# Seven-product weight sums formed by adding transfers in device memory instead of on VectorE, in all four feed-forward layers of a diffusion backbone step

## The chip, the cores and the metric

One core of one Trainium2 chip runs the whole step as one program. The metric is the device time of one execution in microseconds (us); lower is better. Engines are named as in the profile: PE (TensorE matmul), PEld (its weight loads), DVE (VectorE), ACT (ScalarE), POOL (GpSimd) and SP (SyncE, which issues nearly all transfers). Each engine works through its own queue in order and waits at the head of the queue for semaphores of the others.

## The reference

Two layers, 640 tokens (128 context, 512 latent) of width 1024, all in fp32. Each layer is a half-step SwiGLU feed-forward, a mixer (layer 0: a two-dimensional DFT, "Fourier"; layer 1: neighbourhood attention), and a second half-step feed-forward; every part has a norm and a modulation before and after.

```python
def _swiglu(h, w1, w2):
    gate, up = jnp.split(h @ w1, 2, axis=-1)
    return (jax.nn.silu(gate) * up) @ w2

def _half_ffn(x, m, k, g_pre, g_post, w1, w2):
    h = _modulated_prenorm(x, g_pre, m, k)
    return x + 0.5 * m[:, 3 * k + 2, None] * _rmsnorm(_swiglu(h, w1, w2), g_post)

def _fourier_mix(h, w_in, w_out):
    b, s, _ = h.shape
    u = (h @ w_in).reshape(b, s, N_FOURIER_GROUPS, FOURIER_GROUP_DIM)
    f = jnp.fft.fft2(u.astype(jnp.float32), axes=(1, 3), norm="ortho").real
    return f.astype(h.dtype).reshape(b, s, D_MODEL) @ w_out
```

The modulation is `silu(cond) @ w_mod[i] + b_mod[i]`, 2 x 9216 columns over a depth of 1024. D_FF is 2816, 22 "f tiles" of 128.

## The kernel before

**Order of the work.** The program is straight-line: six sub-layers n = 0 to 5, of which n = 0, 2, 3 and 5 are the feed-forward layers (`ffn`), n = 1 is the Fourier mixer (`fourier`) and n = 4 the attention. A list `units` holds all weight tiles (128 x 1024 fp32, 512 KB) in the order of use. `unit(i)` sends up to unit i+3: `send` issues a load on SP into one of four `raw` buffers and splits it into a `hi` part (ACT, line 260) and a `lo` part (DVE, line 261), in six pairs of `hi`/`lo` buffers. Every product is three matmul passes (`mm3`, lines 274 to 276).

**Seven products.** For most f tiles (`w1_fast`) the product of the hidden states with the gate and up columns is formed in Winograd's manner: the weights are four 512-column blocks (two of the gate, two of the up, called `one` and `two` in the code), the tokens two halves, and seven block products take the place of eight. `combine` forms the sums on the token side once per layer. The weight sums are formed for each f tile on DVE inside `send`: kinds `"sums"` and `"again"` by three additions of 512 columns (lines 228 to 230), kind `"all"` by one more (line 243). The gate and the up tile stay in `raw` buffers from their load to their last sum. After every four fast tiles a slice of the second matrix follows (`w2`, five token tiles).

**Background jobs.** The modulation columns are 128 jobs (`gemv`, line 478): one load of 512 KB and two DVE instructions each. `BEHIND` says how many run after `w2` passes of a layer (36, 0, 36, 36, 0, 8); 4 more run in the last slice of n = 0 and 8 inside `fourier` (three in `pair_in(1)`, five between `channels`).

**Fourier.** Its input and output weights are folded on DVE as they are loaded (lines 237 and 238, 16 units). Position sums and channel sums alternate on PE (`positions`, `channels`), each with its split on ACT and DVE between them.

Of the kernel before, what the change touches and what calls it, by code (L numbers as in the profile page):

```python
# [18 lines left out]
P = 128  # L19
# [24 lines left out]
BEHIND = (36, 0, 36, 36, 0, 8)  # L44
TURNS = (
# [107 lines left out]
class Kernel:  # L153
# [59 lines left out]
    def send(self, kind, src):  # L213
# [18 lines left out]
        elif kind.startswith("fold"):  # L232
            raw = self.raw_tile(src)
            a, b = raw[:, one], raw[:, two]
            if "rows" not in kind:
                a, b = a.rearrange("p (m c) -> p m c", m=4)[:, :, 2:], raw[:, 520:].rearrange("p (m c) -> p m c", m=4)
            nc.vector.tensor_tensor(b, a, b, op=ALU.subtract)
            nc.vector.scalar_tensor_tensor(out=a, in0=a, scalar=2.0, in1=b, op0=ALU.mult, op1=ALU.subtract)
        elif kind == "up":
            raw = self.fast["up"]  # L240
        else:
            raw, at = self.fast["gate"], two
            nc.vector.scalar_tensor_tensor(out=raw[:, two], in0=self.fast["sums"][:, two], scalar=-1.0,
                                           in1=raw[:, two], op0=ALU.mult, op1=ALU.subtract)
        n = at.stop - at.start
        if kind in ("block", "foldblock", "foldrowsblock"):
# [4 lines left out]
        return hi, lo  # L251

# [360 lines left out]
    def chain(self, n, i, pss, acc=()):  # L613
# [66 lines left out]
        with high():  # L680
# [33 lines left out]
            if n == 0:  # L714
                j, n_pieces = tiles[0], 2 * len(tiles)
                y = self.staged[:, 2 * j : 2 * j + n_pieces][:, :: -1 if j == CTX_TILE else 1]
# [4 lines left out]
                if i in (1, 2):  # L721
                    v, t, col = (2, SPECIAL, TOK + 1) if i == 1 else (5, 0, TOK)
                    for c in range(0, NCH, 2):
                        hi, lo = (h.block(part, c, 0)[:, :, col] for part in range(2))
                        self.split(hi, lo, self.staged[:, v, c : c + 2, t])
# [13 lines left out]
    def ffn(self, layer, which, base, boundary):  # L739
# [45 lines left out]
        def combine(step):  # L785
# [16 lines left out]
            if step < 2:  # L802
                t = combine.now[k] = [self.temp(("square", "total")[step]).rearrange(shape, **sizes) for _ in range(2)]
                steps = ((1, t[0], b12, b11), (2, t[1], b22, t[0]))
            else:
                t = combine.now[k]
                steps = ((3, t[0], b22, b12), (4, t[1], t[1], b21))
            for i, to, a, b in steps:
                if k == 0:
                    sums[i] = [quad(self.ring(F32R)) for _ in range(2)]  # L810
                nc.vector.tensor_tensor(to, a, b, op=ALU.subtract)
# [37 lines left out]
        def w1_fast(f, ahead):  # L849
# [28 lines left out]
            with high():  # L878
                tt(a, a, w, op=ALU.add)
# [10 lines left out]
            with high():  # L890
                nc.vector.scalar_tensor_tensor(out=q, in0=w, scalar=-1.0, in1=q, op0=ALU.mult, op1=ALU.subtract)
# [24 lines left out]
        def w2(s, tiles):  # L916
# [7 lines left out]
            for a0, f in [(a, f) for a in range(2) for f in range(f0, f1)] if ends else [(None, f) for f in range(f0, f1)]:  # L924
                w = self.unit(base + w2_at[s] + f - f0)
                if n == 0 and s == len(SLICES) - 1 and tiles[0] == 0 and f < f0 + 4:
# [23 lines left out]
        for op, a, half in plan:  # L950
# [7 lines left out]
            elif op == "combine":  # L958
                combine(a)
            elif op == "first":  # L960
# [809 lines left out]
```

## Time and profile before

| | before |
|---|---|
| median of 3 runs (lowest to highest) | 2219.53 us (2216.15 to 2219.59) |
| the profiled execution's own time | 2218.44 us |
| its span, first to last instruction | 2216.7 us |
| mean granted TensorE clock | 0.988 |
| moved by transfers | 293.25 MB, mean 132 GB/s |

The profiled execution lies 1.1 us under the median. Its time is 1.7 us more than its span. A busy PE is not a PE at its peak: matmuls are pipelined, and at half clock a busy PE does half the work, so the granted clock has to be read beside the busy share.

### The profile page before, as it was taken

The numbers are of one execution on the slowest core, as the hardware profiler recorded it, in microseconds if no ns is written. First come the engines' busy times: TensorE is split into PE (matmuls) and PEld (weight loads), VectorE is DVE, ScalarE is ACT, GpSimd is POOL, SyncE is SP. The second block draws the span as 40 slices with busy tenths as digits, with TensorE's granted clock in tenths as the row PEclk, the third lists the DMA queues.
The fourth block names the chain that finished last, engine by engine and source line by source line (L and its number), as shares of the span: only waits on it lengthen the run. The fifth ranks groups of instructions, "written<-read, shape, count | busy, mean of one in ns | idle before, by whom it ended". The sixth has DMA issues, their size and how long they took to land.

```text
span 2216.7 us, 34573 instructions
## 1 busy us (share of the span) xinstructions
PE 2173.2 (98%) x13299; PEld 1997.3 (90%) x13299; DVE 1743.1 (79%) x3218; ACT 1179.2 (53%) x2221; POOL 45.3 (2%) x95
## 2 busy tenths in 40 slices
PE   7999999999899999999999999999999999999998
PEld 5999999977699999898998999989998899999997
DVE  5988898889798889878998898686556686766684
ACT  4544545464654545446544454466778654455452
POOL 0000000010100000001000000010000000000000
PEclk9999999998999999999999999999999999999999
DMA  8244344625324434452344444533333323322242
GB/s 315 86 143 162 134 152 139 216 86 178 116 96 138 159 132 147 148 196 99 109 147 146 141 143 146 179 99 101 111 101 110 119 81 105 115 95 77 95 129 100
DMA packets 85861, 293.25 MB, mean 132 GB/s; under 512 B 9696, under 2 KB 14656, under 8 KB 85568
## 3 DMA queue, kind: packets, MB, share of 16 engines
q1 hardware_dynamic: 85152, 290.39, 39.1%
q8 instruction: 104, 1.70, 0.3%
q10 hardware_dynamic: 544, 0.66, 0.1%
q14 instruction: 61, 0.50, 0.1%
HBM read 275.49 MB, written 11.58 MB: 130 GB/s over the span
## 4 chain that ended last, share of the span: by engine, by line
PE 89%; DVE 5%; ACT 3%; DMA 2%; issue 1%; POOL 0%; SPq 0%; DVEq 0%; POOLq 0%; ACTq 0%
PE main L275 12%; PE main L276 12%; PE main L274 12%; PE score L275 7%; PE score L276 7%; PE score L274 7%; PE turn L275 4%; PE turn L274 4%; PE sum L274 4%; PE sum L275 4%; PE turn L276 4%; PE sum L276 4%; DVE junk L478 1%; DMA raw<-in_w_mod_t 1%; PE sum L1569 1%
## 5 line engine op out<-in xcount | busy, mean ns | idle before, releaser
L260 ACT ACTIVATE hi<-raw 128x1024 fp32r<-128x1024 f32 (+1 forms) x388 | 371.1, 969 | 287.3 <-PE score L275 93.1
L261 DVE TENSOR_TENSOR lo<-raw,hi 128x1024 fp32r<-128x1024 f32 (+1 forms) x388 | 429.7, 1112 | 99.1 <-ACT hi L260 97.7
L274 PE MATMUL main<-hi,ring 128*128 128x512 f32 (+4 forms) x1089 | 412.3, 380 | 5.9 <-ACT hi L260 2.3
L275 PE MATMUL main<-lo,ring 128*128 128x512 f32 (+4 forms) x1089 | 410.8, 378 | 4.8 <-DVE lo L261 4.8
L276 PE MATMUL main<-hi,ring 128*128 128x512 f32 (+5 forms) x1089 | 410.3, 377 | 0.0
L478 DVE SCALAR_TENSOR_TENSOR junk<-raw,wide 128x1024 bf16<-128x1024 f32 x256 | 313.1, 1223 | 79.6 <-DMA raw<-in_w_mod_t 75.5
L276 PE MATMUL score<-ring,lo 128*128 128x320 f32 x916 | 283.4, 309 | 0.6 <-DVE lo L261 0.6
L275 PE MATMUL score<-ring,hi 128*128 128x320 f32 x916 | 283.7, 310 | 0.0
L274 PE MATMUL score<-ring,hi 128*128 128x320 f32 x916 | 283.3, 309 | 0.0
L274 PEld LDWEIGHTS main<-hi,ring 128*128 128x128 f32 (+2 forms) x1089 | 204.9, 189 | 47.9 <-ACT hi L260 3.6
L275 PEld LDWEIGHTS main<-lo,ring 128*128 128x128 f32 (+2 forms) x1089 | 205.9, 189 | 43.9 <-DVE lo L261 6.3
L276 PEld LDWEIGHTS main<-hi,ring 128*128 128x128 f32 (+2 forms) x1089 | 206.0, 189 | 40.5 <-issue 1.2
L274 PE MATMUL turn<-ring,hi 128*128 128x320 f32 x672 | 207.6, 309 | 3.0 <-ACT ring L260 2.9
L275 PE MATMUL turn<-ring,hi 128*128 128x320 f32 x672 | 208.3, 310 | 0.0
L274 PE MATMUL sum<-ring,hi 128*128 128x320 f32 x672 | 208.0, 310 | 0.1
L275 PE MATMUL sum<-ring,hi 128*128 128x320 f32 x672 | 207.8, 309 | 0.0
L276 PE MATMUL sum<-ring,lo 128*128 128x320 f32 x672 | 207.5, 309 | 0.0
L276 PE MATMUL turn<-ring,lo 128*128 128x320 f32 x672 | 207.0, 308 | 0.0
L942 ACT ACTIVATE y<-main 128x512 f32<-128x512 f32 x160 | 94.2, 591 | 208.2 <-PE main L276 207.0
L274 PEld LDWEIGHTS score<-ring,hi 128*128 128x128 f32 x916 | 172.4, 188 | 1.1
L276 PEld LDWEIGHTS score<-ring,lo 128*128 128x128 f32 x916 | 172.2, 188 | 1.0 <-DVE lo L261 1.0
L275 PEld LDWEIGHTS score<-ring,hi 128*128 128x128 f32 x916 | 172.3, 188 | 0.7
(318 smaller groups left out, 4138.8 us busy)
## 6 DMA issues: line engine op xcount, KB each, us to landing
raw<-in_w SPq DMA_DIRECT2D x272, 512.0 KB, 3.7
raw<-in_w_mod_t SPq DMA_DIRECT2D x128, 512.0 KB, 3.5
raw<-in_qkv SPq DMA_DIRECT2D x26, 512.0 KB, 3.5
spill<-ring SPq DMA_DIRECT2D x12, 640.0 KB, 3.3
ring<-spill SPq DMA_DIRECT2D x12, 640.0 KB, 7.4
raw<-in_bias SPq DMA_DIRECT2D x16, 448.0 KB, 3.7
first<-in_w_mod_k SPq DMA_DIRECT2D x8, 512.0 KB, 8.2
ring<-in_w_mod_k SPq DMA_DIRECT2D x8, 512.0 KB, 10.2
```

The costliest lines, as they stand in the source:

```text
L260: a = self.nc.scalar.activation(hi, src, AF.Copy)
L261: self.last_split = a, self.nc.vector.tensor_tensor(lo, src, hi.bitcast(F32), op=ALU.subtract)
L274: mm(out, whi, xhi, start=start, stop=False)
L275: mm(out, whi, xlo, start=False, stop=False)
L276: self.latest = mm(out, wlo, xhi, start=False, stop=stop)
L478: last = self.nc.vector.scalar_tensor_tensor(out=self.junk, in0=raw, scalar=1.0, in1=self.wide[:, cond, :], op0=ALU.mult, op1=ALU.mult, ac ...
L942: nc.scalar.activation(place(i, a), ps[a], AF.Copy)
L1569: mm = nc.tensor.matmul(out, cache_v[:, ds] if k is None else v[c // 2][c % 2][:, slot, ds], probs, start=n == 0, stop=n == len(tiles) - 1)
```

## The change

For every fast tile that is not of kind `"again"` (17 in n = 0, 18 in each of n = 2, 3 and 5: 71 of 79) the four DVE additions go away. In their place POOL issues transfers within device memory: four plain copies of 512 columns (256 KB) into a scratch tensor `far`, then four transfers that add (gate + up block, up + up block, then the sum of three, then the sum of all four). A 16-byte transfer ahead of them, which reads a tile that ACT has just written, holds the group back to its place, five f tiles ahead. The loads of the sums then come from `far`: per f tile SP issues the gate tile, two sums (512 KB), two pieces of 256 KB for the up unit, and a half tile for `"all"`.

The Fourier input fold moves: eight background jobs in n = 0 load the tile, fold it on DVE and write it back through POOL, and `fourier` loads folded tiles. The eight jobs inside `fourier` go; in n = 0 one job runs after each fast tile from f = 5 on. Signs of the token sums change, a column of the context order moves so that eight small splits go away, splits inside `fourier` get high priority, one bank changes.

```diff
+FAR = (0, 2, 3, 5)
...
+        elif kind == "pieces":
+            raw = self.raw.tile([P, UNIT], F32, tag="raw", name=self.name("raw"))
+            for a, piece in zip((one, two), src):
+                nc.sync.dma_start(out=raw[:, a], in_=piece)
+        elif kind == "half":
+            raw, at = self.raw_tile(src, 512), one
...
+    def fold_in(self, k):
+
+        raw = self.raw_tile(self.io["four_in"][k])
+        a, b = (t.rearrange("p (m c) -> p m c", m=4) for t in (raw[:, :512], raw[:, 520:]))
+        self.fold(a[:, :, 2:], b)
+        self.nc.gpsimd.dma_start(out=self.folded[k], in_=raw)
+
+    def far_sums(self, n, f, stage, passed):
+
+        one, two = slice(0, 512), slice(512, UNIT)
+        w1 = self.io["w1"][n // 3, n % 3 // 2, f] if (n, f) in self.far else None
+        put, add = self.nc.gpsimd.dma_start, partial(self.nc.gpsimd.dma_start, accum_op=ALU.add)
+        while w1 is not None and self.staged_sums.get((n, f), 0) <= stage:
+            t, at = self.far[n, f].rearrange("p (a k) -> p a k", a=4), self.staged_sums.get((n, f), 0)
+            if at == 0:
+                put(out=t[:1, :, :1], in_=passed[:1, 0, :4].bitcast(F32).unsqueeze(2))
+                for a, src in enumerate((w1[0][:, one], w1[0][:, one], w1[1][:, one], w1[0][:, two])):
+                    put(out=t[:, a], in_=src)
+            elif at == 1:
+                add(out=t[:, 2], in_=w1[1][:, two])
+                add(out=t[:, 0], in_=w1[1][:, one])
+            elif at == 2:
+                add(out=t[:, 1], in_=t[:, 2])
+            else:
+                add(out=t[:, 3], in_=t[:, 1])
+            self.staged_sums[n, f] = at + 1
...
             elif op == "combine":
                 combine(a)
+                if a == 3:
+                    for stage in range(4):
+                        for f in range(7 if stage < 3 else 6):
+                            self.far_sums(n, f, stage, sums[4][0])
...
             elif op == "fast":
                 w1_fast(a, half)
+                for i in range(4):
+                    self.far_sums(n, a + 5 - i, i, g[a])
+                if n == 0 and a > 4:
+                    self.behind()
...
+                            self.units.append({"sums": ("plain", t[:, :UNIT]), "all": ("half", t[:, UNIT + 512 :]),
+                                               "up": ("pieces", (t[:, UNIT : UNIT + 512], w1[v, 1][:, 512:]))}[op])
...
-                if p and k % 3 == 1:
-                    self.behind()
...
-            self.behind((2, 2, 1, 0)[m])
...
+        for k in range(NCH):
+            self.background.insert(6 + 13 * k // 2, partial(self.fold_in, k))
```

DVE, in the middle of the last feed-forward layer (n = 5), one fast tile from its first sum with the y product to its second hidden half. Before (`sums` and `raw` are the weight tiles in fp32, `left` and `right` the results):

```order
L871 TENSOR_TENSOR left_19973<-score_18368,left_19970 128x320
L875 TENSOR_TENSOR left_20005<-left_19973,turn_19952 128x320
L261 TENSOR_TENSOR lo_20060<-raw_20057,hi_20059 128x1024
L879 TENSOR_TENSOR left_20005<-left_20005,sum_20008 128x320
L228 TENSOR_TENSOR sums_20110<-raw_20096,raw_20108 128x512
L229 TENSOR_TENSOR raw_20108<-raw_20108 128x512
L230 TENSOR_TENSOR sums_20110<-raw_20096,raw_20108 128x512
L261 TENSOR_TENSOR lo_20087<-raw_20084,hi_20086 128x1024
L886 TENSOR_TENSOR right_20006<-left_19973,turn_19952 128x320
L261 TENSOR_TENSOR lo_20099<-raw_20096,hi_20098 128x1024
```

Now:

```order
L906 TENSOR_TENSOR left_20655<-score_18966,left_20652 128x320
L910 TENSOR_TENSOR left_20687<-left_20655,turn_20633 128x320
L295 TENSOR_TENSOR lo_20742<-raw_20739,hi_20741 128x1024
L914 TENSOR_TENSOR left_20687<-left_20687,sum_20690 128x320
L295 TENSOR_TENSOR lo_20778<-raw_20775,hi_20777 128x1024
L921 TENSOR_TENSOR right_20688<-left_20655,turn_20633 128x320
L922 TENSOR_TENSOR right_20688<-right_20688,right_20653 128x320
L295 TENSOR_TENSOR lo_20790<-raw_20787,hi_20789 128x1024
```

The three additions between the splits are gone, and nothing stands in their place on DVE.

POOL, between the feed-forward layers. Before, POOL has only small powers (L610, the roots of the norms) and, in the attention, fills; this is where the attention begins:

```order
L610 TENSOR_TENSOR col_9748<-col_9748,power 128x1
L610 TENSOR_TENSOR col_9756<-col_9756,power 128x1
L1311 MEMSET rms_14462 64x128 x2
L610 TENSOR_TENSOR col_13681<-col_13681,power 128x1
L610 TENSOR_TENSOR col_13695<-col_13695,power 128x1
```

Now, in the second feed-forward layer (n = 2), the group of one f tile (`far_111`) between its neighbours, with the semaphores that each row waits for (DMASW are those of POOL's own transfers):

```order
L275 DMA far_111<-ring_7080 4x1x1 [waits Activation_49]
L284 DMA far_110<-far_110 128x512 [waits DMASW7_49,DMASW4_49]
L277 DMA far_111<-in_w 128x512 [waits DMASW0_49]
L277 DMA far_111<-in_w 128x512 x2
L277 DMA far_111<-in_w 128x512 [waits DMASW5_49]
L280 DMA far_111<-in_w 128x512 [waits DMASW2_49]
L279 DMA far_111<-in_w 128x512 [waits DMASW4_49]
L282 DMA far_111<-far_111 128x512 [waits DMASW7_49,DMASW3_49]
L284 DMA far_111<-far_111 128x512 [waits DMASW5_49,DMASW1_49,DMASW0_49]
L275 DMA far_112<-ring_7220 4x1x1 [waits Activation_49]
```

Although the code asks for one step of four different f tiles at a time, the scheduler has put the nine transfers of one f tile behind each other, each step waiting in POOL's queue for the one before it, and the next f tile's group behind them.

DVE in `fourier`, around the first position sums (`rms`, `left` and `total` are the splits that PE waits for, `lo` the splits of weights, `junk` the modulation jobs). Before:

```order
L261 TENSOR_TENSOR total_5004<-main_4995,square_5003 126x384
L478 SCALAR_TENSOR_TENSOR junk,mod<-raw_5007,wide 128x1024
L237 TENSOR_TENSOR raw_5015<-raw_5015 128x512
L478 SCALAR_TENSOR_TENSOR junk,mod<-raw_5007,wide 128x1024
L238 SCALAR_TENSOR_TENSOR raw_5015<-raw_5015 128x512
L478 SCALAR_TENSOR_TENSOR junk,mod<-raw_5011,wide 128x1024
L261 TENSOR_TENSOR left_5050<-main_5039,left_5049 128x322
L478 SCALAR_TENSOR_TENSOR junk,mod<-raw_5011,wide 128x1024
L261 TENSOR_TENSOR ring_5020<-raw_5015,ring_5019 128x1024
L261 TENSOR_TENSOR ring_4948<-score_5023,ring_4947 128x322
```

Now:

```order
L295 TENSOR_TENSOR total_5276<-main_5267,square_5275 126x384
L257 TENSOR_TENSOR raw_5279<-raw_5279 128x512
L257 TENSOR_TENSOR raw_5329<-raw_5329 128x512
L258 SCALAR_TENSOR_TENSOR raw_5279<-raw_5279 128x512
L258 SCALAR_TENSOR_TENSOR raw_5329<-raw_5329 128x512
L295 TENSOR_TENSOR left_5314<-main_5303,left_5313 128x322
L257 TENSOR_TENSOR raw_5379<-raw_5379 128x512
L295 TENSOR_TENSOR total_5326<-main_5317,square_5325 126x384
L295 TENSOR_TENSOR ring_5284<-raw_5279,ring_5283 128x1024
L295 TENSOR_TENSOR ring_5220<-score_5287,ring_5219 128x322
```

The modulation jobs are gone from between the splits; the folds of the output weights remain.

## Rows read from the trace of the kernel before

**Rows 1.** Page, part 1: busy us of each engine, share of the span.

```profile
PE 2173.2 (98%) x13299; PEld 1997.3 (90%) x13299; DVE 1743.1 (79%) x3218; ACT 1179.2 (53%) x2221; POOL 45.3 (2%) x95
```

**Rows 2.** Stretches of n = 0, 2 and 5: length, busy us, clock, DMA share, GB/s.

```profile
111.00:407.00 296.00, 296.00 (x1757) 275.70 (x1757) 262.54 (x433) 144.43 (x226) 0.00 (x0) 1.00 0.44 145
629.00:999.00 370.00, 369.94 (x2216) 345.83 (x2215) 321.89 (x526) 177.42 (x276) 0.00 (x0) 1.00 0.45 150
1855.00:2146.00 291.00, 291.00 (x1724) 270.85 (x1724) 195.16 (x304) 144.70 (x224) 0.00 (x0) 1.00 0.28 94
```

**Rows 3.** Stretches of 10 us in the Fourier mixer, same columns.

```profile
480.00:490.00 10.00, 6.95 (x25) 5.28 (x26) 9.96 (x18) 3.07 (x3) 0.00 (x0) 0.66 0.33 107
...
520.00:530.00 10.00, 8.23 (x35) 6.74 (x33) 9.97 (x18) 2.31 (x4) 0.00 (x0) 0.67 0.64 215
...
540.00:550.00 10.00, 10.00 (x27) 6.70 (x25) 9.55 (x20) 2.31 (x4) 0.00 (x0) 0.52 0.67 213
550.00:560.00 10.00, 7.65 (x26) 5.79 (x24) 7.04 (x12) 4.76 (x9) 0.00 (x0) 0.80 0.46 157
```

**Rows 4.** Timeline of PE there: start, us, instruction, [idle before, releaser].

```profile
483.05 0.58 PE L275 MATMUL main<-lo,ring 128*128 128x256 f32 x1 [3.37 <-DVE lo L261]
...
522.10 0.39 PE L274 MATMUL main<-hi,ring 128*126 128x256 f32 x1 [1.77 <-DVE rms L261]
...
539.49 0.41 PE L274 MATMUL score<-left,hi 128*128 128x322 f32 x1 [1.85 <-DVE ring L261]
```

**Rows 5.** Waits of PE, 440 to 615 us: total, times, longest.

```profile
PE main L274 <- ACT hi L260: 2.3, 1, 2.3
```

**Rows 6.** Timeline of DVE ahead of two of those stops.

```profile
510.41 1.23 DVE L478 SCALAR_TENSOR_TENSOR junk<-raw,wide 128x1024 bf16<-128x1024 f32 x1 [0.22 <-DMA raw<-in_w_mod_t]
...
537.81 1.22 DVE L478 SCALAR_TENSOR_TENSOR junk<-raw,wide 128x1024 bf16<-128x1024 f32 x1
...
538.95 0.49 DVE L261 TENSOR_TENSOR ring<-score,ring 128x322 fp32r<-128x322 f32 x1
```

**Rows 7.** Groups of DVE by line and form, whole span (count, busy, mean ns).

```profile
L228 DVE TENSOR_TENSOR sums<-raw,raw 128x512 f32<-128x512 f32 x79 | 54.4, 688 | 6.1 <-DMA raw<-in_w 5.7
...
L237 DVE TENSOR_TENSOR raw<-raw 128x504 f32<-128x504 f32 x8 | 5.3, 680 | 2.1 <-DMA raw<-in_four_in 2.1
L238 DVE SCALAR_TENSOR_TENSOR raw<-raw 128x504 f32<-128x504 f32 x8 | 5.3, 680 | 0.1
```

**Rows 8.** Timeline of ACT in n = 5: the first copy of three fast tiles.

```profile
1889.59 0.44 ACT L867 ACTIVATE left<-score 128x320 f32<-128x320 f32 x1 [0.30 <-PE score L276]
...
1901.95 0.44 ACT L867 ACTIVATE left<-score 128x320 f32<-128x320 f32 x1 [0.45 <-PE score L276]
...
1966.73 0.44 ACT L867 ACTIVATE left<-score 128x320 f32<-128x320 f32 x1 [0.22 <-PE score L276]
```

**Rows 9.** DMA issues: queue, count, KB each, median us from issue to landing.

```profile
raw<-in_w SPq DMA_DIRECT2D x272, 512.0 KB, 3.7
...
total<-gate SPq DMA_DIRECT2D x12, 256.0 KB, 3.4
...
x_out<-ring SPq DMA_DIRECT2D x8, 256.0 KB, 2.1
...
wide<-in_cond_rows SPq DMA_DIRECT2D x1, 1024.0 KB, 9.7
...
gate<-rms SPq DMA_DIRECT2D x6, 8.0 KB, 1.8
```

**Rows 10.** POOL's largest group, by line and form.

```profile
L610 POOL TENSOR_TENSOR col<-col,power 128x1 f32<-128x1 f32 x55 | 32.5, 597 | 1568.0 <-DVE col L609 1512.9 <-DVE col L607 55.0
```

**Rows 11.** The busiest 10 us of transfers in a feed-forward layer (columns of rows 2).

```profile
430.00:440.00 10.00, 10.00 (x44) 8.09 (x44) 7.04 (x13) 0.00 (x0) 0.00 (x0) 1.00 0.92 374
```

More of the change, by code (lines that the diff above doesn't have):

```diff
@@ L233, in send @@
             raw = self.raw_tile(src)
[L234 to L238, printed above, removed]
+            self.fold(raw[:, one], raw[:, two])
+        elif kind == "pieces":
[4 more added lines that the diff above has]
+            raw, at = self.raw_tile(src, 512), one
         elif kind == "up":
@@ L242, in send @@
             raw, at = self.fast["gate"], two
-            nc.vector.scalar_tensor_tensor(out=raw[:, two], in0=self.fast["sums"][:, two], scalar=-1.0,
-                                           in1=raw[:, two], op0=ALU.mult, op1=ALU.subtract)
+            nc.vector.tensor_tensor(raw[:, two], self.fast["sums"][:, two], raw[:, two], op=ALU.add)
         n = at.stop - at.start
-        if kind in ("block", "foldblock", "foldrowsblock"):
+        if kind in ("block", "foldblock"):
             hi, lo = (self.ring(F32R)[:, :n] for _ in range(2))
@@ L925, in w2 @@
                 w = self.unit(base + w2_at[s] + f - f0)
-                if n == 0 and s == len(SLICES) - 1 and tiles[0] == 0 and f < f0 + 4:
+                if n == 0 and s == len(SLICES) - 1 and tiles[0] == 0 and f < f0 + 3:
                     self.behind()
@@ L1034, in list_units @@
         self.bases = []
-        self.plans = {}
+        self.plans, self.far, self.staged_sums = {}, {}, {}
         for i in range(DEPTH):
@@ L1053, in list_units @@
                 if i == 0:
-                    self.units += [("foldblock" if k >= NWU else "fold", io["four_in"][k]) for k in range(NCH)]
+                    self.folded = [self.dram.tile([P, UNIT], F32, tag=f"fold{k}", name=self.name("fold")) for k in range(NCH)]
+                    self.units += [("block" if k >= NWU else "plain", self.folded[k]) for k in range(NCH)]
                     self.units += [("plain", io["dft"][k]) for k in range(3)]
-                    self.units += [("foldrowsblock" if u in (3, 4) else "foldrows", io["four_out"][u]) for u in range(NCH)]
+                    self.units += [("foldblock" if u in (3, 4) else "fold", io["four_out"][u]) for u in range(NCH)]
                 else:
@@ L1175, in positions @@
             p = [self.temp("left", F32R)[:, :322] for _ in range(2)]
-            self.split(*p, ps)
+            with high():
+                self.split(*p, ps)
             ps = diffs(m)
             q = [self.temp(kind, F32R)[:126, :384] for kind in ("square", "total")]
-            self.split(*q, ps)
+            with high():
+                self.split(*q, ps)
             return p, q
@@ L1251, in pair_out @@
             boundary(j, far)
+        self.unit(at + 4)
         pair_out(1)
@@ L1726, in host_inputs @@
     small = np.zeros((P, 208))
-    small[:64, :64] = -wave(np.sin, ctx, ctx, CTX) / 128
+    small[:64, :64] = -wave(np.sin, back, ctx, CTX) / 128
     small[:64, 64:128] = -small[:64, :64]
```

47 lines of the change are left out of this document (31 added, 16 removed).

## The prediction

> **What bounds the kernel now.** I read the busy shares first. PE is busy for 2173.2 of 2216.7 us, DVE for 1743.1 [rows 1]. That alone would say that taking work from DVE is worth nothing, so I went on by stretches. In the feed-forward layers PE has no gap at all: 296.00 of 296 us in n = 0, 369.94 of 370 in n = 2, 291.00 of 291 in n = 5, each at full granted clock [rows 2]. DVE is close behind in the first two (262.54 of 296, 321.89 of 370) and far behind in n = 5 (195.16 of 291), where PE is no faster for it. So there, PE is the bound, and a DVE with less to do gives nothing by itself.
>
> The Fourier mixer is the other kind of stage. Between 480 and 560 us DVE is busy for over 9.5 of 10 us in three of the four stretches shown, and PE is the one that stops [rows 3]. The timeline of PE names the stops: 3.37, 1.77 and 1.85 us, each ended by a DVE split [rows 4]. Behind each stop the granted clock falls to the lower of its two levels, 1.2 in place of 2.4 GHz, for part of the stretch: 0.66 after the first, 0.67 after the second, 0.52 and 0.80 after the third [rows 3]. A stop therefore costs twice, once idle and once in slow matmuls. Ahead of the second and third stop DVE was working through modulation jobs of 1.22 us each; the split that PE waited for from 537.6 us on began the moment such a job had ended, at 538.95 [rows 6].
>
> **What the change does to the Fourier mixer.** It takes out eight modulation jobs (16 instructions of 1.22 us, 19.5 us) and eight folds (16 of 0.68 us, 10.9 us [rows 7]): 30 us of DVE in a stage where DVE is what PE waits for. What that is worth I take from the stops, not from the 30 us:
> - Second stop: 1.77 idle, and 10 x (1 - 0.67) = 3.3 us of clock. DVE is full from 504 us on, and four job instructions of 1.22 us stand in that stretch (the row at 510.41 is one), so about 5 us ahead of the split go, more than the stop is long. I take all 5.1.
> - Third stop: 1.85 idle and 4.8 + 2.0 us of clock, a job directly ahead. I take all 8.6.
> - First stop: 3.37 idle and 3.4 us of clock. What is ahead of it on DVE is mostly work of the layer boundary, which stays; five of the folds run earlier, with a gap of DVE after them. I take 2 of 6.8.
> - One wait of 2.3 us for ACT near 560 us [rows 5]: the weight that ACT splits is folded on DVE first, and that fold stays, but DVE reaches it earlier. I take 1.3.
>
> Sum: 5.1 + 8.6 + 2 + 1.3 = 17 us. The lower bound is 0: what comes late next is the round trip PE, ACT, DVE, PE of the position sums, and if it ends where DVE's queue ended before, nothing is gained. The upper bound takes all four in full: 5.1 + 8.6 + 6.8 + 2.3 = 22.8, with some 5 us more if splits at high priority also shorten the stops too small to show here, 28.
>
> **What it does to DVE in the feed-forward layers.** 71 f tiles lose four instructions of 0.69 us [rows 7], the other three lines reading alike, 2.8 us of about 19, 196 us in all. n = 0 gains eight more modulation jobs and eight folds, 20.9 + 10.9 = 32 us, and loses 17 x 2.8 = 47. All of this lies under a full PE, so I cost it at nothing; the cover is the 33 us that DVE has free in n = 0 [rows 2]. Were it gone, n = 0 would be longer by what exceeds it, and the balance is 15 us the other way. Signs of sums cost nothing, the eight small splits less sit in the Fourier stage and are inside the bounds above.
>
> **What it adds: transfers.** Per f tile SP now loads 1.84 MB in place of 1.05, and POOL moves 1.05 MB by copies and 1.05 MB by adding transfers, which read two streams for one written (up to 2.1). A fast tile lasts 12.36 us and a cycle of four with its w2 slice 77.14 us (first copies at 1889.59, 1901.95 and, four tiles on, 1966.73 [rows 8]), so 19.3 us per tile. Two things can go wrong, and neither operation is in the trace of before.
>
> First, *POOL's queue*. Nine transfers per tile stand in it behind each other, and each step waits for the one before. As long as the group takes less than 19.3 us, POOL keeps pace: it starts five tiles ahead, which covers that in the fast phase tiles come every 12.4 us. Above that no lead helps. From below: 16 bytes 1.8 (the 8 KB transfer), the first three copies 2.1 + 2 x 0.7 (256 KB at 374 GB/s [rows 11]), two adding steps of 2.1 each, the last one running under the next tile's first: 9.5 us. From above: 1.8, then 9.7 for four copies (the 1 MB row), two steps at 3.4 (a 256 KB transfer that reads device memory) [rows 9], and nine issues at 0.6 each, since POOL's own short instruction takes that long [rows 10]: 1.8 + 9.7 + 6.8 + 5.4 = 23.7 us. I take the middle, 16.6: the 1 MB row was measured at the crowded start, and the 3.4 us row is itself from a busy queue. That is 2.7 us under the limit, so I cost it at nothing, but the limit lies inside the bounds.
>
> The Trainium skill prices the same thing (DMA: Bandwidth & Descriptors, "Anatomy of one DMA — SWDGE (gpsimd) path": about 2 us per transfer from this queue plus bytes over 436 GB/s). By it the group would take about 11 us, an estimate, and the sum would be the same; no run so far shows such a transfer.
>
> Second, *the 16 DMA engines*. Over a cycle of four tiles n = 0 wants 4 x 1.84 MB of weight sums, 2.1 of w2 and some 13 jobs of 0.52 through SP, 16 to 17 MB, and 8.4 to 12.6 through POOL: 25 to 30 MB in 77.14 us, 325 to 385 GB/s; the busiest stretch of before moved 374 at 92% [rows 11]. n = 2 and 3 want about 290 to 350, n = 5 245 to 300. The mean before was 145, 150 and 94 [rows 2]. A buffer's turn covers delays: each of the four `raw` buffers now serves one unit per tile, so a load of 3.7 us [rows 9] has some 12 us to land, 8 to spare. In n = 0 a modulation job shares the buffers and leaves about 6. I cost it at nothing, with n = 0 as the place where it may show.
>
> **The sum.** 2218.4 - 17 = 2201.4, against the profiled execution, which is 1.1 us under the median of the runs: 2202 us.
>
> **Rivals.**
> - *POOL falls behind (slower than before).* Mechanism: the group of one f tile takes longer than 19.3 us, so the sums' load on SP waits, and with it everything behind it in SP's queue, the w2 tiles and modulation loads too. Each microsecond above costs 71 us. At 20 us it is +50, 2251; at 22 us +192, 2393. It decides against the change from 19.6 us on, where 17 us are eaten. For it: the upper bound of 23.7, and loads that compete for the same engines. Against: the middle of the bounds, and that copies are pipelined. Chance 0.22.
> - A special form of it: a DVE instruction holds up each issue on POOL. If each of the nine waited out one split of 1.22 us, the group would be 11 us longer, 27.6, and the time 2201 + 71 x 8.3 = 2790. I give this 0.02 of the 0.22: DVE's work in a tile is nearly all additions and splits of two inputs, and only the norms use other forms. The Trainium skill has this rule (SBUF — State Buffer, "Who interferes with whom"): DVE's two-port modes lock GpSimd out of the port by which it writes descriptors, and additions of two tensors have no such mode. No run here shows either.
> - *The first layer becomes bound by transfers.* At 385 GB/s wanted and 374 moved, n = 0 would lose about 2 us per cycle, 10 us in all, and a few us at `combine`, where the groups of two to three tiles start together. 2201 + 14 = 2215. Chance 0.10.
> - *Fourier does not get shorter*, since the round trip through ACT and DVE ends where the queue did. 2213 to 2220, gain 0 to 5. Chance 0.08.
>
> **How the numbers follow.** The forecast, 2191 to 2212, has 0.60. Outside it are the transfers-bound first layer (2208 to 2225), no gain in Fourier (2213 to 2220) and POOL behind (2223 and up). From 2188, two under the full upper bound, to 2245, which takes in a group of up to 19.9 us, the range holds 0.60 + 0.10 + 0.08 and a quarter of the last, about 0.8; the forecast's own range is 2191 to 2212. A change of under 0.2% (4.4 us) can't be told from none here. Faster: 0.60, half of the first-layer case and a fifth of the Fourier case, 0.66. Same: the rest of those two, 0.10. Slower: POOL's case and the tail of the first layer, 0.24.
>
> **What would show it.** Right: PE without gaps in all four feed-forward layers, DVE lower there by about 2.8 us per tile; POOL's groups ending before the loads that read them, with waits on POOL mostly for ACT; the stops at 1.77 and 1.85 us gone and the clock at 1.00 between 520 and 560 us. Wrong: SP waiting for POOL's transfers, ACT's `hi` splits waiting for loads from `far`, PE gaps every tile at the end of a layer (POOL late) or in n = 0 alone (engines full), or the Fourier stage stopping as long as before on splits with an idle DVE ahead of them.

## The result, and the profile after

The changed kernel took 2645.64 us, median of 4 runs (2638.99 to 2648.85), against 2218.28 us (2216.15 to 2219.59) for the kernel before: a ratio of 1.1924, 95% interval 1.1896 to 1.1952. I had forecast 2202 us, and gave the case that came 0.22. The page of the changed kernel, busy times and queues, answers to [rows 1]:

```profile
PE 2249.7 (85%) x13299; PEld 2057.9 (78%) x13299; DVE 1585.3 (60%) x2930; ACT 1175.6 (44%) x2217; POOL 473.0 (18%) x742
...
q1 hardware_dynamic: 116976, 350.43, 39.3%
q0 software_dynamic: 67040, 153.14, 28.0%
```

DVE did lose 158 us of work. PE is busy for 76 us more, with the same 13299 matmuls, and idle for 354 us more (2647.1 - 2249.7 against 2216.7 - 2173.2): a stop costs idle time and then slow matmuls. The four feed-forward stretches, in the columns of [rows 2]:

```profile
111.00:590.00 479.00, 338.61 (x1888) 312.19 (x1887) 269.35 (x443) 154.99 (x243) 93.32 (x141) 0.83 0.78 216
785.00:1299.00 514.00, 442.18 (x2493) 407.71 (x2492) 325.61 (x541) 211.70 (x357) 112.39 (x172) 0.93 0.77 218
1309.00:1835.00 526.00, 443.89 (x2469) 406.14 (x2468) 315.75 (x531) 204.51 (x349) 111.64 (x172) 0.92 0.78 211
2150.00:2620.00 470.00, 411.35 (x2374) 381.76 (x2373) 235.56 (x368) 195.25 (x312) 108.49 (x164) 0.94 0.73 194
```

None of them has a full PE or a full granted clock now, and DVE is far from full too: nothing that computes is the bound. Both kernels issue the same number of matmuls in the same order of stages, so the start of the same matmul by number in two traces says how much later a stage ended. This table is worked out so, for every kernel of this study: us gained (-) or lost against the profiled run of the kernel before, by stage.

```
                     n = 0  Fourier   n = 2   n = 3  attention  n = 5    all
changed kernel       171.5    -21.4    93.7   111.7      1.6     73.4   430.2
p2_no_far             19.4    -12.8     0.8     0.4      0.0     -0.3     7.5
p3_no_put            147.4    -20.0    70.4    79.5      0.1     39.8   316.5
p4_in_turns          142.2    -19.2    88.1   126.4      2.3     64.6   403.7
q1_half_all           86.8    -20.5    19.0    25.0      0.0      2.3   112.3
q2_half_first         83.7    -20.3     1.6    -0.2      1.6     -0.3    66.2
q3_lead              118.0    -19.1    51.4    80.6      1.7     26.8   258.8
r1_fold_by_sp        113.2    -21.3    89.3   110.5     -0.9     68.5   358.9
r2_half_fold_sp       62.1    -20.0     0.0    -0.2      1.7     -0.3    43.3
r3_no_far_fold_sp     19.2    -11.9     1.5     0.4      1.5     -0.3    10.3
r4_folds_only         15.6      1.9    -0.1    -0.4      0.1      0.0    17.1
s1_jobs_only           7.0    -14.6     0.2    -0.2      0.1     -0.3    -8.3
s2_jobs_in_w2         24.0    -16.8    -0.1    -0.2      1.8     -0.3     8.7
u1_lead_early         91.9    -19.7    37.2    61.3      0.2     13.0   183.6
```

(Stages end at the matmuls that start at 440, 625, 1055, 1480 and 1750 us after the span's start in the kernel before. Each row is one profiled execution, which can lie some us off the median of its runs: 2331.34 against 2323.57 us for q1_half_all. The experiments below carry these names.) So the Fourier mixer gained what I forecast, and the feed-forward layers lost 450 us. The timeline of POOL in n = 2 shows with what (start, us, instruction, what it waited for):

```profile
968.96 0.83 POOL L284 DMA_DIRECT2D far<-far  x1 [5.46 <-DMA far<-far]
969.49 0.84 POOL L275 DMA_DIRECT2D far<-ring  x1
976.23 2.10 POOL L277 DMA_DIRECT2D far<-in_w  x4 [5.90 <-DMA far<-ring]
982.47 0.87 POOL L280 DMA_DIRECT2D far<-in_w  x1 [4.14 <-DMA far<-in_w]
984.38 0.84 POOL L279 DMA_DIRECT2D far<-in_w  x1 [1.03 <-DMA far<-in_w]
992.07 0.81 POOL L282 DMA_DIRECT2D far<-far  x1 [6.85 <-DMA far<-in_w]
997.87 0.81 POOL L284 DMA_DIRECT2D far<-far  x1 [4.98 <-DMA far<-far]
998.39 0.82 POOL L275 DMA_DIRECT2D far<-ring  x1
```

One group of nine, from 969.49 to the next at 998.39: 28.9 us where a tile has 19.3 [rows 8]. POOL itself works 6.3 us of it; the rest is waiting, five times, for the transfer before to land. The mean distance from a tile's first copy to the next tile's, from the fourth group of a layer on, is 29.4, 26.2, 27.3 and 24.8 us in n = 0, 2, 3 and 5. By these means, what 14 distances have above 14 x 19.3 is 96, 112 and 76 us in n = 2, 3 and 5: the table has 93.7, 111.7 and 73.4. There the account closes. (By itself that shows only that groups and tiles went at one rate. That POOL set it is read from its waits: among these 14 groups it waited for ACT's signal once in n = 2, 10.0 us, and never in n = 5.) Who waits for the groups in n = 2, from the view of SP's waits (total, times, longest):

```profile
SPq L204 <- DMA far<-far: 117.0, 10, 38.7
```

and, behind SP, from the view of all waits there:

```profile
ACT hi L294 <- DMA raw<-far: 102.8, 18, 17.3
```

In n = 0 the same distances make 13 x 10.1 = 131 us, and 171.5 were lost. But there the distances are not the length of the groups alone, since three of them hold a wait of POOL for ACT of 21 to 22 us:

```profile
POOL far L275 <- ACT ring L294: 65.1, 3, 22.3
```

SP's waits from 110 to 580 us name another releaser, the write of a folded weight, which stands in POOL's queue behind the group of a tile and holds one of the four `raw` buffers until it has landed:

```profile
SPq L239 <- DMA fold<-raw: 84.5, 3, 30.0
SPq L204 <- DMA fold<-raw: 46.8, 4, 20.2
```

### The profile page after: what moved, and what is told of

Read it like the earlier page. It is cut to its first block, busy times and chain, and to the rows that moved or that the text cites. A ratio compares the mean times of both kernels' runs of the same rounds, so it can differ in the third digit from the quotient of the medians.

```text
span 2647.1 us, 36033 instructions
## 1 busy us (share of the span) xinstructions
PE 2249.7 (85%) x13299; PEld 2057.9 (78%) x13299; DVE 1585.3 (60%) x2930; ACT 1175.6 (44%) x2217; POOL 473.0 (18%) x742
## 3 DMA queue, kind: packets, MB, share of 16 engines
q1 hardware_dynamic: 116976, 350.43, 39.3%
q0 software_dynamic: 67040, 153.14, 28.0%
## 5 line engine op out<-in xcount | busy, mean ns | idle before, releaser
L294 ACT ACTIVATE hi<-raw 128x1024 fp32r<-128x1024 f32 (+1 forms) x459 | 449.8, 985 | 917.3 <-DMA raw<-far 450.2
L295 DVE TENSOR_TENSOR lo<-raw,hi 128x1024 fp32r<-128x1024 f32 (+1 forms) x459 | 518.1, 1131 | 537.6 <-ACT hi L294 536.6
L308 PE MATMUL main<-hi,ring 128*128 128x512 f32 (+4 forms) x1083 | 409.7, 379 | 4.0 <-ACT main L948 2.1
L310 PE MATMUL main<-hi,ring 128*128 128x512 f32 (+4 forms) x1083 | 404.8, 374 | 0.0
L308 PEld LDWEIGHTS score<-ring,hi 128*128 128x128 f32 x916 | 185.1, 202 | 198.5 <-ACT left L902 146.0
L308 PEld LDWEIGHTS main<-hi,ring 128*128 128x128 f32 (+2 forms) x1083 | 203.2, 188 | 46.0 <-ACT main L948 3.4
L309 PEld LDWEIGHTS main<-lo,ring 128*128 128x128 f32 (+1 forms) x1083 | 203.5, 188 | 42.5 <-DVE lo L295 4.9
L310 PEld LDWEIGHTS main<-hi,ring 128*128 128x128 f32 (+1 forms) x1083 | 203.2, 188 | 39.9 <-issue 0.2
L310 PEld LDWEIGHTS sum<-ring,lo 128*128 128x128 f32 x672 | 131.0, 195 | 96.8 <-DVE lo L295 96.8
L277 POOL DMA_DIRECT2D far<-in_w x284 | 155.8, 607 | 226.9 <-DMA far<-ring 196.8
L308 PEld LDWEIGHTS turn<-ring,hi 128*128 128x128 f32 x672 | 135.5, 202 | 75.4 <-ACT rms L623 41.2
```

The costliest lines, as they stand in the source:

```text
L277: put(out=t[:, a], in_=src)
L294: a = self.nc.scalar.activation(hi, src, AF.Copy)
L295: self.last_split = a, self.nc.vector.tensor_tensor(lo, src, hi.bitcast(F32), op=ALU.subtract)
L308: mm(out, whi, xhi, start=start, stop=False)
L309: mm(out, whi, xlo, start=False, stop=False)
L310: self.latest = mm(out, wlo, xhi, start=False, stop=stop)
```

## The experiments

**What a step of the chain costs by itself (p1_steps).** A kernel that runs only groups, four in each of seven stretches, with other work beside them. Its core (`load` is the stretch's other work):

```diff
+        for n, load in enumerate(stretches):
...
+            gone = nc.gpsimd.tensor_tensor(start, last, power, op=ALU.mult)
...
+            first = nc.vector.tensor_tensor(begun, start, power, op=ALU.mult)
...
+            with self.behind_of(first):
+                load()
+            for f in range(4):
+                with self.behind_of(gone):
+                    far, gone = self.group(n, f, zero)
```

> This kernel computes nothing of the model. It runs the nine-transfer group of one f tile, in the order of the changed kernel, four times in a row in each of seven stretches: with nothing beside it; beside DVE subtractions of 128x1024; beside DVE modulation instructions; beside DVE copies of 128x1024; beside SP loads of 512 KB every 4 us or so; beside SP loads as fast as they go; beside paced loads and subtractions together. Theory A, a fixed landing: each of the five dependent steps takes 5 to 6 us in every stretch, and a group 24 to 28 us even with nothing beside it. Theory B, contention in the 16 DMA engines: a group is 10 to 14 us with nothing or only DVE beside it, and 25 us or more beside SP's loads. Theory C, DVE holds up the issue: 10 to 14 us with nothing or only loads beside it, 25 us or more beside one or all of the three DVE stretches.

Measured, from the starts on POOL's timeline: us from one group's 16-byte transfer to the next group's, second and third distance of each stretch.

```
nothing beside it                 23.5  22.7
DVE subtractions                  22.8  23.8
DVE modulation instructions       23.1  22.7
DVE copies of 128x1024            24.8  24.0
SP loads, paced                   24.9  25.7
SP loads, as fast as they go      35.4  34.9
paced loads and subtractions      26.9  25.4
```

A group with nothing beside it, in the timeline:

```profile
73.45 0.81 POOL L1735 DMA_DIRECT2D far<-zero  x1
78.36 2.13 POOL L1737 DMA_DIRECT2D far<-in_w  x4 [4.10 <-DMA far<-zero]
82.12 0.86 POOL L1739 DMA_DIRECT2D far<-in_w  x1 [1.64 <-DMA far<-in_w]
84.65 0.86 POOL L1738 DMA_DIRECT2D far<-in_w  x1 [1.68 <-DMA far<-in_w]
```

and two of the stretches (us; DVE, ACT and POOL busy; clock, DMA share, GB/s), with nothing beside the groups and with SP's loads at full rate:

```profile
50.70:96.00 45.30, 0.00 (x0) 0.00 (x0) 11.49 (x18) 1.00 0.51 93
...
700.00:745.00 45.00, 0.00 (x0) 4.79 (x24) 7.19 (x11) 1.00 1.00 326
```

Theory A holds, just under its 24 to 28 us: the chain takes 23 us with idle engines around it, above the 19.3 of a tile. Contention adds 2 us beside paced loads and 12 beside a full load. DVE's subtractions and modulation instructions add nothing, its copies 1 to 2 us, so theory C falls. The Trainium skill's rule of it (SBUF — State Buffer, "Who interferes with whom") names copies among the instructions that can lock GpSimd out; in this stretch they ran back to back at 0.69 us each, and nothing like a lock for their whole length is seen: nine issues that each waited one out would make a group 6 us longer. And by the Trainium skill's fit for a transfer of this queue (DMA: Bandwidth & Descriptors, "Anatomy of one DMA — SWDGE (gpsimd) path") I had estimated a group at 11 us; the measurement is twice that.

**Everything but the sums by transfer (p2_no_far).**

```diff
-FAR = (0, 2, 3, 5)
+FAR = ()
```

> No sums by transfer: FAR is empty, so DVE forms the sums again in all four layers; everything else of the change stays (folds and eight jobs moved into the first layer, Fourier stage without them). If the 17 us that I forecast for the Fourier mixer are right and the 32 us of added DVE work in n = 0 are hidden: 2201 us, 2190 to 2212. DVE in n = 0 would then be busy for about 295 of 296 us, so the rival is that n = 0 becomes DVE-bound and gives 5 to 15 us back: 2206 to 2216. If the Fourier stage is not shorter: 2213 to 2220. The long groups on POOL are gone in any case, so by none of them is it over 2235.

2225.73 us, ratio 1.004 (1.0029 to 1.0051). n = 2, 3 and 5 stand within 0.8 us of before, so summing on DVE costs nothing there, and all of the 450 us but some 20 in n = 0 belong to the sums by transfer and the queue they stand in. n = 0 lost 19 us to the work moved into it, more than the 5 to 15 that I gave for it, and the Fourier mixer gained 12.8 us in place of the 21.4 of the changed kernel. That n = 0 lost them to DVE's time is not shown; the runs of folds alone and jobs alone below speak against it.

**The 16-byte transfer (p3_no_put).**

```diff
-                put(out=t[:1, :, :1], in_=passed[:1, 0, :4].bitcast(F32).unsqueeze(2))
-                for a, src in enumerate((w1[0][:, one], w1[0][:, one], w1[1][:, one], w1[0][:, two])):
-                    put(out=t[:, a], in_=src)
+                gone = self.nc.gpsimd.tensor_tensor(self.col(1), passed[:, 0, :1].bitcast(F32), self.power[:, :1], op=ALU.mult)
+                with self.behind_of(gone):
+                    for a, src in enumerate((w1[0][:, one], w1[0][:, one], w1[1][:, one], w1[0][:, two])):
+                        put(out=t[:, a], in_=src)
```

> The 16-byte transfer that paces each group is replaced by one 128x1 instruction of POOL that reads the same tile, with the copies queued behind it; the other eight transfers and their order in the group stay. Theory A (chain of dependent landings): a group loses the 6 us between the 16-byte transfer and the first copy, 27.5 to about 21.5 us; with the excess over 19.3 us per tile going from 8.2 to 2.2 us, 445 us of loss become about 120, 2320 us (2280 to 2380). Theory B (the bytes fill the DMA engines): 16 bytes less change nothing, 2600 to 2650. Theory C (each issue held up by DVE): one issue less of nine, 2.5 to 3 us per group, 2450 to 2520.

2535.20 us in one run: 110 us better, far from the 325 of theory A and above the number of C, which the stretches above exclude. None of the three had it. The groups' distance went from 26.2 to 24.6 us in n = 2, not to 21.5. Sixteen bytes hardly cost anything themselves. In the run of groups alone the copies behind them began 4.4 to 5.5 us after their issue (7.3 to 8.4 beside SP's full load) where the last add of the group before was just ahead of them, and 1.9 to 2.5 us after it at the head of six stretches, where nothing was. They waited in the queue for that add; without them the copies do (behind an add on its way, the first copy landed after it 48 times of 48). The account still closes: 14 x (24.6 - 19.3) = 74 us, and n = 2 lost 70.4.

**The same transfers, not waiting for each other (p4_in_turns, q3_lead, u1_lead_early).** POOL's order is changed so that the steps of four tiles alternate.

```diff
+            with self.behind_of(self.beat(passed)):
                 if at == 0:
-                    put(out=t[:1, :, :1], in_=passed[:1, 0, :4].bitcast(F32).unsqueeze(2))
...
+    def beat(self, passed):
+        if self.fast.get("passed") is not passed:
+            self.fast["passed"] = passed
+            self.fast["gone"] = self.nc.gpsimd.tensor_tensor(self.col(1), passed[:, 0, :1].bitcast(F32), self.power[:, :1], op=ALU.mult)
+        return self.fast["gone"]
```

> As the run without the 16-byte transfer, and POOL's order is staggered: behind the one paced instruction of each fast tile stand the four copies of f + 5, the two adds of f + 4, the add of f + 3 and the last add of f + 2, so that each transfer waits for one that was issued a whole tile earlier. The same bytes, the same eight transfers per tile, the same DVE and SP work. Theory A: no wait of over a microsecond or two is left on POOL but the one for ACT, PE is without gaps again, 2195 to 2230 us. Theory B: the engines have the same bytes to move, so little changes, 2550 us or more. Theory C: eight issues of which each waits out a DVE instruction fit under 19.3 us, so it too would give 2200 to 2250 here, and the run of the steps alone has to tell it from A.

2615.83 us, ratio 1.1783 (1.1751 to 1.1815), which looks like theory B. But POOL now sat idle for its pace, and SP still waited for the last add. All waits of n = 2, and SP's:

```profile
POOL col L291 <- ACT ring L301: 223.7, 14, 29.1
```

```profile
SPq L204 <- DMA far<-far: 142.3, 11, 16.9
```

With a step per tile the last add of tile f is issued only two tiles ahead of its use: I had traded the chain for too short a lead. The next run gives it nine tiles:

```diff
-                    self.far_sums(n, a + 5 - i, i, g[a])
+                    self.far_sums(n, a + 9 - i, i, g[a])
```

(with the first groups of a layer staggered in the same way).

> All sums by transfer, staggered as in the run before, but nine tiles ahead in place of five, so that the last add of a tile is issued behind the paced instruction six tiles earlier and not two. The same bytes and transfers. If what was left in the staggered run was its short lead (SP waited 142 us in n = 2 for the last add): no waits of SP for sums, 2200 to 2290, the most of it in n = 0, where POOL's 10.4 us, SP's 5.3 + 1.5 us and jobs of 4.9 us per tile, by the share that each queue's packets took, are 22 us of all 16 engines in 19.3. If the bytes themselves are too many in all four layers: 2450 or more, with SP's loads slow to land and no wait for sums.

2477.16 us, 1.1174 (1.1151 to 1.1196). SP's waits for the last add in n = 2 fell to 22.3 us, and the groups' distance to 15.5 us there and 15.0 in n = 5, below the 19.3 of a tile (17.3 in n = 3, and 20.0 in n = 0): outside n = 0 the same transfers of the same bytes keep pace when they don't wait for each other. The longer lead was not run with the chained order; in n = 2 and 5 POOL hardly waited for its signal there, so it would have had little to give. Some 259 us of loss were left, much of it in stops at the first f tiles of a layer. Starting n = 2, 3 and 5 earlier, and writing the folds from SP:

```diff
                 w1(a, half)
+                if n and half == 0 and 0 in a:
+                    first_sums(g[0])
```

> All sums by transfer, staggered and nine tiles ahead as before, with two edits more: in n = 2, 3 and 5 the first groups are issued when the layer's first tile has been through its first half, some 40 us earlier than at the combination of the input sums; and the folds are written from SP's queue. If the late start was the rest of the loss: n = 5 loses under 5 us in place of 27, n = 2 under 25 in place of 51, n = 3 under 45 in place of 80, n = 0 60 to 100; together 2290 to 2370. If the DMA engines have too many bytes: n = 2 and n = 3 lose the same as before or nearly so, 2400 to 2470.

2397.30 us, 1.0804 (1.0776 to 1.0832), between the two ranges: the late start was a part of it only. The two stretches of n = 2, while POOL's transfers run and after they are done:

```profile
707.00:950.00 243.00, 221.80 (x1237) 202.86 (x1236) 164.67 (x265) 101.45 (x157) 86.42 (x132) 0.95 1.02 285
1000.00:1100.00 100.00, 100.00 (x607) 94.04 (x606) 75.18 (x120) 50.39 (x78) 0.00 (x0) 1.00 0.58 193
```

The 16 DMA engines are full (1.02) at 285 GB/s and PE stops; when the sums are done they are at 0.58 and PE has no gap. The view of DMA issues gives the median time of a plain weight load from issue to landing, 7.9 us in the first stretch and 4.3 in the second (4.0 in n = 2 of the kernel before):

```profile
raw<-in_w SPq DMA_DIRECT2D x21, 512.0 KB, 7.9
...
raw<-in_w SPq DMA_DIRECT2D x14, 512.0 KB, 4.3
```

So I read theory B as the second bound, behind the chain, though no run changed the bytes alone: n = 2 and 3 came out between the two theories' numbers.

**Every second tile (q1_half_all, q2_half_first).**

```diff
-                        elif op == "gate" and n in FAR:
+                        elif op == "gate" and n in FAR and v % 2:
...
-                        elif n in FAR and op in ("sums", "up", "all") and (n, v, "again") not in self.plans:
+                        elif n in FAR and v % 2 and op in ("sums", "up", "all") and (n, v, "again") not in self.plans:
```

> Sums by transfer for every second f tile only (the odd ones), in all four layers; the even ones are summed on DVE as before. A group of nine transfers has two tiles, 38.6 us, and takes 25 to 28. If the length of the group against the tile's time is what cost 427 us, PE is without gaps in n = 2, 3 and 5 again, and the time is 2218 - 20 for the Fourier stage plus what n = 0 loses to DVE (25 us with no sums by transfer, 32 us of added work against 25 us taken away here, so 0 to 15): 2198 to 2215. If any load that comes from sums by transfer is late by itself (a landing behind which SP's queue stands), half the tiles keep half the loss: 2350 to 2450.

2323.57 us, 1.0478 (1.0460 to 1.0495), between the two ranges. n = 5 lost 2.3 us of 73, n = 2 and 3 19 and 25 of 94 and 112: the dose fits the chain against two tiles' time, with a rest in n = 2 and 3 that I have not traced. Half the tiles are half the bytes too, so this run does not tell the chain from the bytes. n = 0 kept 87, which the number did not allow for.

> The same in n = 0 alone; n = 2, 3 and 5 sum on DVE under a full PE. By the theory that PE hides DVE's sums in those layers and that only n = 0 needs relief: the same as with all four layers halved, within 5 us, 2198 to 2215. If the sums on DVE cost something in n = 2, 3 and 5 after all, it is slower than the run with all layers halved by over 5 us.

2285.13 us, 1.0307 (1.0292 to 1.0323), `FAR = (0,)` with the same edit. It is 38 us faster than the last, neither the same nor slower: sums by transfer in n = 2, 3 and 5 had nothing to give.

**The folds' queue (r1_fold_by_sp, r2_half_fold_sp, r3_no_far_fold_sp).**

```diff
-        self.nc.gpsimd.dma_start(out=self.folded[k], in_=raw)
+        self.nc.sync.dma_start(out=self.folded[k], in_=raw)
```

> The changed kernel with one word different: the eight folded weights are written to device memory from SP's queue, not from POOL's, where each stood behind the group of an f tile and held one of the four raw buffers until it had landed (SP waited 131 us for that in n = 0). If that wait is a cause of its own: n = 0 loses about what n = 2 loses to the groups alone, 95 us in place of 172, and the whole is 2540 to 2600 us; n = 2, 3 and 5 stay as they were. If n = 0 is held by its groups and the wait for the fold only stands where another would: 2630 to 2650.

2583.52 us, 1.1651 (1.1623 to 1.1679): n = 0 lost 113.2 in place of 171.5, and n = 2, 3 and 5 what they lost before, within 5 us. It is a cause of its own, 58 us. And what is left in n = 0 is now the groups: SP waits there for their adds,

```profile
SPq L204 <- DMA far<-far: 77.0, 9, 17.7
```

POOL waits for ACT once only (7.7 us) among the distances that count, which have a mean of 28.4 us, and 13 x (28.4 - 19.3) = 118 us is near the 113.2.

> Every second f tile of n = 0 alone summed by transfer, and the folds written from SP's queue. Without the latter n = 0 lost 84 us, 45 of them beside SP waiting for folds. If both causes are named rightly: the 45 go and some of the rest, n = 0 loses 10 to 40, Fourier gives 19.5 back: 2208 to 2240. If the sums by transfer are late even with two tiles of time: 2260 to 2285.

2256.97 us, 1.0176 (1.0154 to 1.0198): 22 us of the 45 went, and n = 0 still lost 62. It lies between the two ranges, and the first was too hopeful; what holds n = 0 with half the sums and no folds in POOL's queue is not settled.

> No sums by transfer, folds written from SP's queue. In the run with no sums by transfer n = 0 lost 25 us, of which 24 us of SP's waits were for folds that had no other transfer ahead of them on POOL (4 us from issue to landing each). If DVE, at 32 us more, is what n = 0 is short of, this stays within 5 us of 2226. If the hold of the raw buffers is: 2205 to 2215.

2227.58 us, 1.0034 (1.0019 to 1.0050): as without this edit. Where POOL's queue is empty, the queue of the folds is no matter.

**What the Fourier mixer gained from (r4_folds_only, s1_jobs_only, s2_jobs_in_w2).** First the folds alone: DVE's sums and the folds' writes from SP as in the last run, the jobs back in the mixer as below, and one background job in n = 0 after every second fast tile, not after every one, with the folds closer together among them.

```diff
             for k in range(NCH):
+                if p and k % 3 == 1:
+                    self.behind()
                 even_in(k, token(k, 256 * p, 256 * p + P), es)
...
+            self.behind((2, 2, 1, 0)[m])
             self.unit(at + 3 + m)
```

> No sums by transfer, folds in n = 0 written from SP, but the eight modulation jobs back in the Fourier mixer where they stood: 11 us of DVE moved in place of 32. If the gain in Fourier follows the DVE time taken out (19 of 30 us): about 7 us there, and n = 0 loses under 5 (it has 33 us free of DVE and 11 are asked): 2210 to 2218. If the jobs ahead of the splits, as I read the stops, were the whole of Fourier's loss: no gain there, 2218 to 2224.

2233.74 us, 1.0074 (1.0057 to 1.0091): the mixer is 1.9 us longer, not 7 shorter, and n = 0 pays 15.6 for the folds. The folds alone gain nothing. Then the jobs alone: the kernel before, with the two calls of `behind` in the mixer taken out and one edit:

```diff
                 w1_fast(a, half)
+                if n == 0 and a in range(5, 20, 2):
+                    self.behind()
```

> The kernel before with one edit: the eight modulation jobs of the Fourier mixer run in n = 0, one after each second fast tile. No folds moved, no sums by transfer. If the jobs were all of Fourier's loss: that stage is 19 us shorter, n = 0 loses what 20 us of DVE cost there. Folds without jobs cost 18 us there and both together 26, so the jobs should cost about 8: 2218 - 19 + 8 = 2207, 2198 to 2214. If the gain needed the folds gone too, 5 to 10 us in Fourier, 2214 to 2222.

2210.11 us in 6 runs (2207.84 to 2214.06), ratio 0.9962, 0.9948 to 0.9975: 0.4% faster than the kernel before. The mixer gives 14.6 us, n = 0 takes 7.0. Its waits of PE from 440 to 620 us no longer have the rows for `rms` and `score` on DVE, 1.8 and 1.9 us in the kernel before; the wait of [rows 5] for ACT, 2.3 us, is still there.

> The same eight jobs, spread over the w2 slices of n = 0 with the 36 that run there (44 in place of 36), where DVE has more time than in the fast tiles. If it is DVE's time in the fast tiles that costs: 3 to 6 us less than with one job after each second fast tile, 2196 to 2208. If the raw buffers or SP's queue cost: the same within 3 us.

2224.80 us, 1.0022 (1.0012 to 1.0031): the same jobs among the `w2` slices, where I read more free time on DVE, cost n = 0 24.0 us in place of 7.0. Both numbers that I gave were wrong. PE waits for ACT's split, 9.0 us in four stops, and ACT, by the view of its waits in n = 0, for the sums on DVE:

```profile
ACT hi L260 <- DVE sums L230: 52.8, 14, 6.5
```

In the kernel before this wait is 33.5 us, with the jobs behind the fast tiles 18.0. DVE's free time by its sum is not what decides; where a job's load stands among the weights of the next tile is my reading, which I did not test further.

## Why the prediction was wrong, by its own steps

- **The bound, and DVE's sums at nothing:** right. With DVE's sums kept, n = 2, 3 and 5 stayed within 0.8 us of the kernel before.
- **The Fourier mixer, 17 us with bounds 0 to 28:** right, 21.4. The stops at the second and third place of [rows 4] and the wait of [rows 5] are gone; the first stayed, as half expected, at 3.2 us for 3.37. Windows of the changed kernel at the three places (columns of [rows 3]) show the clock at full level behind the last two:

```profile
650.00:660.00 10.00, 6.82 (x37) 6.09 (x36) 8.41 (x11) 2.11 (x2) 0.00 (x0) 0.83 0.51 178
...
690.00:700.00 10.00, 10.00 (x59) 8.31 (x59) 9.12 (x16) 4.30 (x8) 0.00 (x0) 1.00 0.25 87
700.00:710.00 10.00, 10.00 (x47) 7.40 (x46) 7.96 (x14) 5.44 (x10) 0.00 (x0) 1.00 0.62 202
```

  I credited jobs and folds together. The jobs alone gave 14.6 and 16.8 us, the folds alone nothing. Both together gave 12.8 and 11.9 where DVE formed the sums and 19 to 21 in the runs with sums by transfer in n = 0; why the two differ I have not traced.
- **"I take the middle, 16.6: ... so I cost it at nothing":** this is the step that failed. With nothing beside it a group takes 23 us, in the kernel 24.8 to 27.3 (means of n = 2, 3 and 5), where 19.3 were allowed. Two terms were short. The adds at 2.1 to 3.4 us took 4.7 to 6.3. The 16 bytes at 1.8 us took 4.3 (median of the run of groups alone), and with that an overlap was wrong: the last add was to run under the next tile's first transfer at no cost, but the 16 bytes landed behind it every time, so its length stood in the chain. The upper bound of 23.7, added up from rows of plain transfers, covers the group alone and not the group beside the kernel's loads. The rival had the mechanism and its price per microsecond nearly right: at 7 us above, 2201 + 71 x 7 would be 2700, and it came to 2646. The first groups of each layer are made ahead, so that 13 or 14 distances of 17 or 18 count; the folds' writes, which it did not have, are in the 2646 too.
- **The 16 engines at 374 GB/s:** wrong too, though it did not decide. Full engines moved 285 GB/s with adding transfers among them (326 beside SP's full load in the run of groups alone), and beside those 285 GB/s a load that was to land in 3.7 us took 7.9. By the reading above this is the bound behind the chain.
- **32 us of DVE in n = 0 under 33 us of cover:** wrong by 19 us where DVE kept its sums (p2_no_far). The cost did not follow DVE's time: 11 us of folds cost n = 0 15.6 us, 20 us of jobs 7.0 or 24.0 by their place. Cover by the sum of free time does not say when it is free; what n = 0 paid for is not settled.
- **What I left out:** the eight folds' writes, listed with DVE's work and not with POOL's queue, cost 58 us behind the groups there. The prediction asked which queue a transfer is moved past, and did not ask it of these.
- **DVE's hold-up of the issue, 0.02 of the chance:** its number, 27.6 us, came near the groups' distance by accident. Its ground was incomplete, since the modulation jobs are neither additions nor splits, but beside subtractions or modulation instructions a group is as long as beside nothing.

## What to carry to other kernels

Price transfers that depend on each other by their steps from issue to landing, 4.3 to 6.3 us each here (medians of the run of groups alone), and not by their bytes alone: the bytes of an add of 256 KB keep the 16 engines busy for 1.4 us, an estimate from 128 packets of 178 ns. Compare that chain with the time that its consumer takes per tile, and stagger the chains of several tiles before counting on a lead. List for each queue everything that is put into it, the small writes too, and the buffers that they hold. Test the parts of a change apart: the eight jobs alone were worth 0.4%, and were buried under the rest.

## What the runs showed of the hardware that I had not expected

- **Adding transfers take the DMA engines about twice as long per byte.** The packet records of the changed kernel's trace: 2048-byte packets of the adding transfers last 178 ns (median), plain ones of 2048 bytes on SP's queue 84 ns, and 4096-byte packets 159 ns on both queues. On the page, 153.14 MB on POOL's queue took 28.0% of the engines' span and 350.43 MB on SP's 39.3%: 207 against 337 GB/s at full use.
- **POOL's queue landed in order, and a tiny transfer waits for it.** A transfer of 16 bytes took 1.6 us at the least and 8.1 at the most in the run of groups alone, by what was ahead of it and beside it. Issued behind an add on its way (21 times) it landed 0.16 to 0.35 us after that add each time, and no transfer of that run landed before one issued ahead of it on POOL. The view of its line, with the count, the durations on POOL and the time to landing:

```profile
L1735 POOL DMA_DIRECT2D far<-zero x28: 574/813/1409, 2.2 to 891.5; - x28
...
DMA to landing us min/median/max: 1.6/4.3/8.1
```
